# Logits of a two-layer decoder trunk: the products with the low half of the keys move from 64 to 128 rows, and the forget gates' bias rows move into them

## The chip, the core and the metric

The kernel runs on one core of one Trainium2 chip. The metric is the device time of one execution in microseconds. One execution in which every engine was recorded gives the profile; times in the rows below are microseconds from the start of its span.

## What is computed

Two layers over 512 tokens of width 1024, all in fp32. A layer sends `u = LN(x)*(1+scale)+shift` through one wide projection whose columns feed four mixers (pooling, a short convolution, and two attentions of four heads of 64 channels each), gates and sums their branch projections, projects once more, and adds an MLP of width 4096. The change concerns the logits of the two attentions:

```python
# MoBA: with 512 tokens, blocks of 256 and top 3, all past blocks are chosen: plain causal attention
logits = einsum('bhqd,bhkd->bhqk', rotary(q), rotary(k)) * 64 ** -0.5      # masked above the diagonal
# FoX: the same without rotary, plus a bias from the forget gates
cum = cumsum(log_sigmoid(u @ w_f + b_f))
logits = einsum('bhqd,bhkd->bhqk', q, k) * 64 ** -0.5 + cum[:, None] - cum[None, :]
p = softmax(logits); y = einsum('bhqk,bhkd->bhqd', p, v)
```

## The kernel before

**Products.** TensorE multiplies operands rounded to fp32r. To keep fp32's accuracy each operand is split into hi (rounded) and lo (the rest), and a product is three matmuls, hi*hi, hi*lo and lo*hi, into one PSUM bank: `mm3`, lines L128 to L130. `split` (L122 on ScalarE, L123 on VectorE) makes the halves.

**Order.** A layer's projections run tile by tile, 24 matmuls for 128 output columns. Between tiles, pieces of other work are emitted from Python generators: `between_step(rate)` takes the next piece of the attention or of the forget gates, `ada_step(rate)` the next piece of the modulation vectors (VectorE, L316 and L318). Layer by layer: first projections (queries and keys of MoBA, queries of FoX), values and rotary of MoBA, then tiles of convolution and pooling and the eight gate tiles of branch 0 with the MoBA attention between them; then FoX's values, forget gates and keys; then 16 gate tiles of branches 1 and 2 with the FoX attention between them; then branch 3, the output projection and the MLP. A scheduler orders each engine's instructions when the program is built, by the order in which they are written and by its own estimate of when operands and buffers are there; the queues then run in that order.

**Buffers.** Most tiles of 4 KB a partition come from one pool, `unit()`, of 24 buffers. A tile whose buffer is still read by older work waits.

**Logits.** `stack_queries` puts hi of a head's queries on the head's own 64 partitions and lo on the other 64. `stack_keys` puts hi of the keys on both halves, so that one matmul over 128 rows (L558) sums two of the three products. It puts lo of the keys on the head's own half only; one tile holds lo for two pairs of heads. The third product (L564) runs over 64 rows. A bf16 product of the identity and a mask (L559) adds the causal mask. In FoX a matmul over 32 rows (L562) adds the bias: `forget_rows` makes, for each head, 32 rows of which four hold the cumulated log gates and ones, for queries and for keys, by transposes into two PSUM banks and two copies (L684). Per tile of 128 queries of one head there are n = 256, 256, 384 and 512 key columns for the four query tiles. A layer has 16 such tiles in MoBA and 16 in FoX.

Behind a tile's logits stand the maximum (L566, VectorE), the exponential (L568, ScalarE), the normalization (L569, L571), transposes of the probabilities (L580, TensorE), their split, and the products with the values (L592, L593).

Of the kernel before, what the change touches and what calls it, by code (L numbers as in the profile page):

```python
# [30 lines left out]
UNITS = 24  # L31
# [9 lines left out]
EARLY_V = 0  # L41
# [26 lines left out]
def decoder_kernel(ctx, tc, x, c, positions, w_ada, b_ada, w_in, b_in, w_pool, pool_scale, conv_w,  # L68
# [5 lines left out]
    class Engine:  # L74
        """an engine whose instructions keep the order in which they are written while its letter is pinned"""
# [56 lines left out]
    def load(dst, src):  # L132
        """the loads of the start are issued in the order in which they are written, all others after them"""
        ins = nc.sync.dma_start(dst, src)
        if ordered[0]:
            tc.keep_in_program_order(ins)
            ordered[1] = ins.ins.name
        else:
            tc.add_manual_dep(ins.ins, ordered[1], mybir.DependencyInfo(
                mybir.DependencyClass.NoSync, mybir.DependencyReason.DATA), reason="after the start")  # L140
        return ins
# [25 lines left out]
    # silu(c), one column per k-tile  # L167
# [9 lines left out]
    def mean_rstd(xt, sums):  # L177
        """-mean and 1/std of the rows of xt, whose parts sum to sums"""
        nmean, rstd = small(), small()
        if len(sums) == 2:  # L180
            V.tensor_scalar(nmean, sums[0], sums[1], -1.0 / D, op0=ALU.add, op1=ALU.mult)  # L181
        else:
            V.tensor_scalar(nmean, sums[0], -1.0 / D, None, op0=ALU.mult)
        S.activation(t2(1024, BF16), xt, AF.Square, bias=nmean, accum_out=rstd)  # L184
        return nmean, rstd
# [5 lines left out]
    def statistics(xt, by_act):  # L191
        """mean, variance and 1/std of the rows of a tile"""
        if by_act:
            s0, mean, rstd = small(), small(), small()
            S.activation(t2(1024, BF16), xt, AF.Identity, scale=-1.0 / D, accum_out=s0)
            S.activation(t2(1024, BF16), xt, AF.Square, bias=s0, accum_out=rstd)
            V.tensor_scalar(mean, s0, -1.0, None, op0=ALU.mult)
            finish_rstd(rstd)
            return mean, rstd
        st, mv, rstd = small(12, "bn"), small(2, "mv"), small()  # L200
        for h in range(2):
            V.bn_stats(st[:, 6 * h:6 * h + 6], xt[:, HALF[h]])
        V.bn_aggr(mv, st.rearrange("p (a b) -> p a b", a=2))
        V.tensor_scalar(rstd, mv[:, 1:2], EPS, None, op0=ALU.add)
        G.tensor_tensor(rstd, rstd, mhalf, op=ALU.pow)
        return mv, rstd
# [25 lines left out]
    # per-partition columns of biases and scales  # L232
# [42 lines left out]
    # rotary tables  # L275
# [88 lines left out]
    # work that is emitted between the tiles of the projections  # L364
# [29 lines left out]
    def norm_tail(xt, gb, bb, ps):  # L394
        """xt <- LN(ALPHA * xt + psum) * gb + bb; returns the sums of its halves"""
        sums = [small(), small()]
        for h in range(2):
            cs = HALF[h]
            V.scalar_tensor_tensor(xt[:, cs], xt[:, cs], ALPHA, ps[h], op0=ALU.mult, op1=ALU.add,
                                   accum_out=sums[h])  # L400
        nmean, rstd = mean_rstd(xt, sums)
        t = unit()
        V.scalar_tensor_tensor(t, xt, nmean, gb, op0=ALU.add, op1=ALU.mult)
        finish_rstd(rstd)
        sums = [small(), small()]
        for h in range(2):
            cs = HALF[h]
            V.scalar_tensor_tensor(xt[:, cs], t[:, cs], rstd, bb[:, cs], op0=ALU.mult, op1=ALU.add,
                                   accum_out=sums[h])
        return sums  # L410
# [41 lines left out]
    def col_weights(w, c0, n=256):  # L452
        """hi/lo of n columns as n/128 stationary tiles, one at a time"""
        raw = load_raw((KD, n), [(lambda r: r, kcols(w, c0, n))])
        for j in range(n // P):
            t = whl((2, KD, P))
            split(t[:, 0], t[:, 1], raw[:, :, j * P:(j + 1) * P])
            yield t

    def project(w, tiles, evac, nh):  # L460
        """tiles: list of 256-wide column starts; evac(index of 128-tile, psum)"""
# [30 lines left out]
    def token_values(l, c0, n):  # L492
        """token-major projection of n columns (256 or 260) plus bias"""
# [26 lines left out]
    # for the logits of a head, hi and lo of its queries lie on the two halves of the partitions (hi on the head's own)  # L520
    # and hi of its keys on both: a pass over all partitions sums two of the three products
# [10 lines left out]
    def stack_keys(src, lo, bias=None):  # L532
        kt = unit((P, 2, T), F32R)
        for hh in range(2):
            own, other = OWN[hh], OWN[1 - hh]
            for half in (own, other):
                if bias is None:
                    S.copy(kt[half, hh], src[own])
                else:
                    S.activation(kt[half, hh], src[own], AF.Identity, bias=bias[own])  # L540
            if bias is None:
                V.tensor_tensor(lo[own], src[own], rd(kt[own, hh]), op=ALU.subtract)
            else:
                V.scalar_tensor_tensor(lo[own], src[own], bias[own], rd(kt[own, hh]), op0=ALU.add, op1=ALU.subtract)
        return kt, lo

    def attention(qk, v2, bias, ys):
        """causal attention of four heads, a piece for each step of the generator"""

        def logits(pr, hh, i):  # L550
            q, (kt, kl) = qk[pr], qk[2 + pr]
            h = 2 * pr + hh
            hp = slice(64 * hh, 64 * hh + 64)
# [6 lines left out]
            if bias is not None:  # L560
                hb = slice(32 * h, 32 * h + 32)
                TE.matmul(sps[:, :n], bias[0][hb, qc], bias[1][hb, :n], start=False, stop=False,  # L562
                          tile_position=(32 * h, 0))
            TE.matmul(sps[:, :n], q[hp, hh, qc], kl[hp, :n], start=False, stop=True)  # L564
# [20 lines left out]
        def values(pr, hh, half, pts, av):  # L585
            """the stationary operand is hi and lo of the values: the products of lo come out on the other partitions"""
# [48 lines left out]
    def forget_rows(z, cqk):  # L635
# [38 lines left out]
        V.tensor_copy(stq[:, :, :, 0], h4)  # L674
        V.tensor_tensor(stq[:, :, :, 1], c4, h4, op=ALU.subtract)
# [3 lines left out]
        res = unit((P, 2, T), F32R)  # L679
        for a in range(2):  # L680
            ps = bank("tr")
            for i in range(NT):
                TE.transpose(ps[:, i * P:(i + 1) * P], stg[:, a, i].rearrange("p h c -> p (h c)"), ident)
            S.copy(res[:, a], ps)  # L684
            cqk[a] = res[:, a]
            yield

# [53 lines left out]
    # ================= start =================  # L741
    def first_projection(w, tiles, evac):
        """K-outer projection of up to six 128-column tiles, each k-tile of u made on the way"""
# [6 lines left out]
        def load_ada(k0, g):  # L750
            """columns of g k-tiles of the shift and of the scale, all rows"""
# [122 lines left out]
    for l in range(DEPTH):  # L874
        pending += [ada_chunk(l, ch) for ch in (2, 3, 4)]
        # ---- MoBA projections, rotary and attention
        qk = [None] * 4

        qf2, klo = [None] * 2, [None]
# [8 lines left out]
        def rotate():  # L888
# [10 lines left out]
            for n, idx in enumerate(order):  # L899
# [13 lines left out]
                else:  # L913
                    if klo[0] is None:
                        klo[0] = unit((P, 2, T), F32R)
                    qk[idx] = stack_keys(qf, klo[0][:, idx - 2])
                yield

        fqk, fklo = [None] * 4, [None]

        def fox_evac(idx, ps):
# [4 lines left out]
            else:  # L926
                if fklo[0] is None:
                    fklo[0] = unit((P, 2, T), F32R)
                fqk[idx] = stack_keys(ps, fklo[0][:, idx - 2], cl[:, 14 + idx:15 + idx])
# [37 lines left out]
        # ---- pool  # L967
# [41 lines left out]
        # ---- conv: columns c_c, c_h, c_b  # L1009
# [38 lines left out]
        # ---- gates and branch projections  # L1048
# [35 lines left out]

        if EARLY_V:
            between_flush()
            v2, z = token_values(l, 2304, 260)
            cqk = [None, None]
            between.append(forget_rows(z, cqk))
# [3 lines left out]
        # ---- FoX projections and attention  # L1093
        between_flush()
        ada_rate[0] = ADA_IN
        if not EARLY_V:
            v2, z = token_values(l, 2304, 260)
            cqk = [None, None]
            between.append(forget_rows(z, cqk))
        project(w_in[l], [2048], lambda i, ps: fox_evac(i + 2, ps), 0)  # L1100
        between_flush()
        between.append(attention(fqk, v2, cqk, y_fox))
# [9 lines left out]
        # ---- W_o, norm, modulation of the MLP input  # L1112
# [10 lines left out]
        # ---- MLP  # L1123
# [78 lines left out]
```

## Time and profile before

| | us |
|---|---|
| three runs, lowest / median / highest | 1642.57 / 1645.42 / 1645.82 |
| span of the profiled execution, first to last instruction (nothing is shown around it) | 1642.6 |
| busy: TensorE matmuls / weight loads | 1609.2 (98%) / 1320.2 (80%) |
| busy: VectorE / ScalarE / GpSimd | 993.6 (60%) / 729.3 (44%) / 50.5 (3%) |

Matmuls overlap in the pipeline: a matmul's recorded duration is longer than the time for which it keeps the next one from starting. How much of the stream it takes is read from start to start. PE is TensorE, DVE is VectorE, ACT is ScalarE, POOL is GpSimd.

### The profile page before, as it was taken

How to read it: one execution, taken by the hardware profiler on the slowest of the kernel's cores; microseconds unless marked ns; L12 is line 12 of the kernel's file. 1: busy time of each engine (PE TensorE's matmuls, PEld its weight loads, DVE VectorE, ACT ScalarE, POOL GpSimd, SP SyncE). 2: the span in 40 equal slices, each digit the busy share in tenths (PEclk: the TensorE clock that was granted, in tenths of full speed). 3: DMA queues.
4: the chain of work that ended last, by engine and by line, in shares of the span. 5: the costliest groups of instructions: out<-in, count | busy, mean ns of one | idle time of the engine just before them, and what ended most of it. 6: DMA issues, size and time to landing. Idle time of an engine off the chain costs nothing.

```text
span 1642.6 us, 19902 instructions
## 1 busy us (share of the span) xinstructions
PE 1609.2 (98%) x7647; PEld 1320.2 (80%) x7647; DVE 993.6 (60%) x1629; ACT 729.3 (44%) x1210; POOL 50.5 (3%) x154
## 2 busy tenths in 40 slices
PE   5999999999999999999999999999999999999998
PEld 4877887778888888888888788777888988888886
DVE  7897455676675445744678835677567632265454
ACT  4565444443374434412375543554334643352231
POOL 1000000000010000000010000000000100000000
PEclk9999999999999999999999999999999999999999
DMA  9625222544536554222624222444226442332241
GB/s 318 187 75 177 81 87 82 181 129 135 200 108 193 167 166 154 103 79 101 241 92 151 95 90 65 148 147 146 73 83 231 141 123 83 103 103 94 86 180 51
DMA packets 151298, 215.54 MB, mean 131 GB/s; under 512 B 7564, under 2 KB 112991, under 8 KB 151203
## 3 DMA queue, kind: packets, MB, share of 16 engines
q1 hardware_dynamic: 148723, 206.84, 38.9%
q0 software_dynamic: 2176, 7.14, 1.1%
q8 instruction: 60, 0.98, 0.2%
q14 instruction: 35, 0.29, 0.1%
q10 hardware_dynamic: 304, 0.28, 0.1%
HBM read 205.33 MB, written 8.91 MB: 130 GB/s over the span
## 4 chain that ended last, share of the span: by engine, by line
PE 69%; issue 20%; DVE 4%; DMA 2%; ACT 2%; POOL 1%; SPq 0%; POOLq 0%; ACTq 0%; DVEq 0%
PE ps_mm L128 16%; PE ps_mm L130 16%; PE ps_mm L129 16%; PE ps_br L129 2%; PE ps_br L128 2%; PE ps_br L130 2%; PE ps_S L129 2%; PE ps_S L128 2%; PE ps_S L130 2%; PE ps_tr L130 2%; PE ps_tr L129 2%; PE ps_tr L128 2%; PE ps_S L564 1%; PE ps_tr L580 1%; DMA raw<-in_w_in_dram 1%
## 5 line engine op out<-in xcount | busy, mean ns | idle before, releaser
L128 PE MATMUL ps_mm<-uT,whl 128*128 128x512 f32 (+1 forms) x1280 | 492.3, 385 | 0.0
L130 PE MATMUL ps_mm<-uT,whl 128*128 128x512 f32 (+1 forms) x1280 | 487.4, 381 | 0.0
L129 PE MATMUL ps_mm<-uT,whl 128*128 128x512 f32 (+1 forms) x1280 | 486.9, 380 | 0.0
L123 DVE TENSOR_TENSOR whl<-raw,whl 128x1024 fp32r<-128x1024 f32 (+1 forms) x218 | 269.9, 1241 | 242.3 <-ACT whl L122 236.3
L122 ACT CAST whl<-raw 128x1024 fp32r<-128x1024 f32 (+1 forms) x218 | 229.9, 1058 | 180.9 <-PE ps_br L130 139.9
L130 PEld LDWEIGHTS ps_mm<-uT,whl 128*128 128x128 f32 x1280 | 240.9, 188 | 47.4
L128 PEld LDWEIGHTS ps_mm<-uT,whl 128*128 128x128 f32 x1280 | 241.1, 188 | 46.4 <-issue 0.7
L129 PEld LDWEIGHTS ps_mm<-uT,whl 128*128 128x128 f32 x1280 | 241.3, 189 | 45.1
L318 DVE SCALAR_TENSOR_TENSOR unit<-aw,scol,unit 128x512 f32<-128x512 f32 x148 | 110.8, 749 | 87.3 <-DMA aw<-in_w_ada_dram 86.4
L1067 ACT ACTIVATE t<-ps_mm,hgate 128x512 f32<-128x512 f32 x64 | 44.1, 690 | 202.2 <-PE ps_mm L130 202.2
L1128 ACT ACTIVATE t<-ps_mm,cols 128x512 f32<-128x512 f32 x62 | 42.7, 689 | 186.0 <-PE ps_mm L130 186.0
L716 DVE TENSOR_TENSOR raw<-raw,unit 128x1024 f32<-128x1024 f32 x80 | 94.6, 1219 | 11.3 <-DMA raw<-in_w_down_dram 5.9
L1075 DVE SCALAR_TENSOR_TENSOR t<-t,ps_br 128x512 f32<-128x512 f32 x48 | 33.0, 688 | 105.2 <-PE ps_br L130 100.1
L128 PE MATMUL ps_mm<-whl,unit 128*128 128x512 f32 x180 | 70.7, 392 | 0.0
L130 PE MATMUL ps_mm<-whl,unit 128*128 128x512 f32 x180 | 70.7, 392 | 0.0
L129 PE MATMUL ps_mm<-whl,unit 128*128 128x512 f32 x180 | 70.5, 392 | 0.0
L122 ACT CAST unit<-unit 128x512 fp32r<-128x512 f32 (+1 forms) x94 | 55.2, 613 | 32.0 <-DVE unit L123 31.8
L123 DVE TENSOR_TENSOR unit<-unit,unit 128x512 fp32r<-128x512 f32 (+1 forms) x94 | 61.8, 679 | 8.3 <-ACT unit L122 8.1
L184 ACT ACTIVATE t<-unit,s 128x1024 bf16<-128x1024 f32 x28 | 32.1, 1147 | 61.2 <-DVE s L181 55.5
L571 ACT ACTIVATE t<-t,s 128x128 f32<-128x128 f32 (+1 forms) x64 | 35.7, 563 | 32.4 <-DVE s L569 32.1
L130 PE MATMUL ps_br<-unit,whb 128*128 128x512 f32 x128 | 50.0, 390 | 0.0
L128 PE MATMUL ps_br<-unit,whb 128*128 128x512 f32 x128 | 49.9, 390 | 0.0
(275 smaller groups left out, 2577.6 us busy)
## 6 DMA issues: line engine op xcount, KB each, us to landing
raw<-in_w_in_dram SPq DMA_DIRECT2D x47, 1024.0 KB, 5.2
aw<-in_w_ada_dram SPq DMA_DIRECT2D x160, 256.0 KB, 2.8
raw<-in_w_up_dram SPq DMA_DIRECT2D x32, 1024.0 KB, 6.0
raw<-in_w_down_dram SPq DMA_DIRECT2D x32, 1024.0 KB, 4.8
unit<-in_w_ada_dram SPq DMA_DIRECT2D x32, 256.0 KB, 5.8
rawb<-in_w_branch_dram SPq DMA_DIRECT2D x32, 256.0 KB, 2.7
raw<-in_w_o_dram SPq DMA_DIRECT2D x8, 1024.0 KB, 4.9
xmid<-unit POOLq DMA_DIRECT2D x12, 512.0 KB, 2.9
```

Of the source, the lines that this page charges most:

```text
L122: S.copy(hi, src)
L123: V.tensor_tensor(lo, src, rd(hi), op=ALU.subtract)
L128: TE.matmul(ps, wh, ah, start=first, stop=False)
L129: TE.matmul(ps, wh, al, start=False, stop=False)
L130: last_mm[0] = TE.matmul(ps, wl, ah, start=False, stop=last)
L184: S.activation(t2(1024, BF16), xt, AF.Square, bias=nmean, accum_out=rstd)
L318: V.scalar_tensor_tensor(a, aw, scol[:, k:k + 1], a, op0=ALU.mult, op1=ALU.add)
L571: S.activation(pr_[:, :nv], pr_[:, :nv], AF.Copy, scale=sm)
L716: V.tensor_tensor(raw[:, k % 2], raw[:, k % 2], grow, op=ALU.mult)
L1067: S.activation(tg, ps, AF.Tanh, bias=hgate[l][:, n * KD + d:n * KD + d + 1], scale=0.5)
L1075: V.scalar_tensor_tensor(tg, tg, 1.0, bp, op0=ALU.add, op1=ALU.mult)
L1128: S.activation(r, ps, AF.Relu, bias=cl[:, B_UP + idx:B_UP + idx + 1])
```

## The change

Lo of the keys gets a tile of its own for each pair of heads, `(P, 2, T)`: for each head all 128 partitions. In MoBA lo is written on both halves, so L564 becomes a 128-row product of the stacked queries with it (which adds the product lo*lo). In FoX lo stays on the head's own half; the other half takes the four key-side bias rows of that head, and the remaining rows are zero or meet zeros. A second stacked tile of queries, `second`, holds hi of the queries on the head's own half and the query-side bias rows on the other half. L562 is left out. `forget_rows` therefore ends with twelve copies of 64 or 32 partitions and four memsets a layer instead of two copies, and it comes behind the keys (`while qk[3] is None: yield`; it was emitted there before, too). The pool gets 25 buffers; the scratch of GpSimd's DMA descriptors is set to 8192.

```diff
-UNITS = 24
+UNITS = 25
...
-    def stack_keys(src, lo, bias=None):
-        kt = unit((P, 2, T), F32R)
+    def stack_keys(src, bias=None):
+        kt, lo = unit((P, 2, T), F32R), unit((P, 2, T), F32R)
...
             if bias is None:
-                V.tensor_tensor(lo[own], src[own], rd(kt[own, hh]), op=ALU.subtract)
+                for half in (own, other):
+                    V.tensor_tensor(lo[half, hh], src[own], rd(kt[own, hh]), op=ALU.subtract)
             else:
-                V.scalar_tensor_tensor(lo[own], src[own], bias[own], rd(kt[own, hh]), op0=ALU.add, op1=ALU.subtract)
+                V.scalar_tensor_tensor(lo[own, hh], src[own], bias[own], rd(kt[own, hh]),
+                                       op0=ALU.add, op1=ALU.subtract)
...
-    def attention(qk, v2, bias, ys):
+    def attention(qk, v2, second, ys):
...
+            q2 = q if second is None else second[pr]
...
             TE.matmul(sps[:, :n], q[:, hh, qc], kt[:, hh, :n], start=True, stop=False)
             TE.matmul(sps[:, qc], identb, maskb, start=False, stop=False)
-            if bias is not None:
-                hb = slice(32 * h, 32 * h + 32)
-                TE.matmul(sps[:, :n], bias[0][hb, qc], bias[1][hb, :n], start=False, stop=False,
-                          tile_position=(32 * h, 0))
-            TE.matmul(sps[:, :n], q[hp, hh, qc], kl[hp, :n], start=False, stop=True)
+            TE.matmul(sps[:, :n], q2[:, hh, qc], kl[:, hh, :n], start=False, stop=True)
...
-    def forget_rows(z, cqk):
+    def forget_rows(z, qk, second):
...
-        V.tensor_copy(stq[:, :, :, 0], h4)
-        V.tensor_tensor(stq[:, :, :, 1], c4, h4, op=ALU.subtract)
+        for hh in range(2):
+            s2 = slice(2 - 2 * hh, 4 - 2 * hh)
+            V.tensor_copy(stq[:, :, s2, 0], h4[:, :, hh::2])
+            V.tensor_tensor(stq[:, :, s2, 1], c4[:, :, hh::2], h4[:, :, hh::2], op=ALU.subtract)
...
-        res = unit((P, 2, T), F32R)
+        while qk[3] is None:
+            yield
         for a in range(2):
             ps = bank("tr")
             for i in range(NT):
                 TE.transpose(ps[:, i * P:(i + 1) * P], stg[:, a, i].rearrange("p h c -> p (h c)"), ident)
-            S.copy(res[:, a], ps)
-            cqk[a] = res[:, a]
+            for pr in range(2):
+                if a == 0:
+                    second[pr] = unit((P, 2, T), F32R)
+                for hh in range(2):
+                    own, other = OWN[hh], OWN[1 - hh]
+                    if a == 0:
+                        S.copy(second[pr][own, hh], rd(qk[pr][own, hh]))
+                        S.copy(second[pr][other, hh], ps[other])
+                    else:
+                        lo = qk[2 + pr][1]
+                        r0 = other.start + 32 * pr
+                        r1 = other.start + 32 * (1 - pr)
+                        G.memset(rd(lo[r1:r1 + 32, hh]), 0.0)
+                        S.copy(lo[r0:r0 + 32, hh], ps[r0:r0 + 32])
             yield
...
-    nc = bacc.Bacc("TRN2", target_bir_lowering=False, num_devices=1)
+    nc = bacc.Bacc("TRN2", target_bir_lowering=False, num_devices=1, dynamic_dma_scratch_size=8192)
```

## Rows read from the trace of the kernel before

**Rows 1.** The page: busy time of TensorE, and its granted clock in 40 slices.
```profile
PE 1609.2 (98%) x7647; PEld 1320.2 (80%) x7647; DVE 993.6 (60%) x1629; ACT 729.3 (44%) x1210; POOL 50.5 (3%) x154
...
PEclk9999999999999999999999999999999999999999
```

**Rows 2.** The waits of TensorE: us in total, times, longest.
```profile
PE ps_tr L170 <- DMA cst<-in_consts_dram: 6.3, 1, 6.3
```

**Rows 3.** By source line, L562 and L564: count, ns minimum/median/maximum, forms.
```profile
L562 PE MATMUL ps_S<-unit x32: 377/408/498, 237.4 to 1150.7; 32*128 32x256 f32 x16, 32*128 32x384 f32 x8, 32*128 32x512 f32 x8
...
L564 PE MATMUL ps_S<-unit,unit x64: 379/410/500, 89.3 to 1151.1; 64*128 64x256 f32 x32, 64*128 64x384 f32 x16, 64*128 64x512 f32 x16
```

**Rows 4.** TensorE in order of time, first FoX logits: start, duration, line.
```profile
237.40 0.38 PE L562 MATMUL ps_S<-unit 32*128 32x256 f32 x1
237.71 0.38 PE L564 MATMUL ps_S<-unit,unit 64*128 64x256 f32 x1
238.03 0.50 PE L128 MATMUL ps_mm<-uT,whl 128*128 128x512 f32 x1
238.36 0.40 PE L129 MATMUL ps_mm<-uT,whl 128*128 128x512 f32 x1
```

**Rows 5.** TensorE in order of time, last FoX logits (fourth head).
```profile
1150.32 0.39 PE L558 MATMUL ps_S<-unit,unit 128*128 128x512 f32 x1
1150.55 0.23 PE L559 MATMUL ps_S<-maskb,identb 128*128 128x128 bf16 x1
1150.71 0.50 PE L562 MATMUL ps_S<-unit 32*128 32x512 f32 x1
1151.13 0.50 PE L564 MATMUL ps_S<-unit,unit 64*128 64x512 f32 x1
1151.56 0.39 PE L592 MATMUL ps_mm<-unit,unit 128*128 128x256 f32 x1
1151.79 0.28 PE L593 MATMUL ps_mm<-unit,unit 128*128 128x256 f32 x1
```

**Rows 6.** TensorE in order of time, last logits of FoX's third head.
```profile
1123.10 0.50 PE L562 MATMUL ps_S<-unit 32*128 32x512 f32 x1
1123.52 0.50 PE L564 MATMUL ps_S<-unit,unit 64*128 64x512 f32 x1
```

**Rows 7.** TensorE in order of time, second MoBA logits.
```profile
94.98 0.23 PE L559 MATMUL ps_S<-maskb,identb 128*128 128x128 bf16 x1
95.14 0.38 PE L564 MATMUL ps_S<-unit,unit 64*128 64x256 f32 x1
```

**Rows 8.** TensorE in order of time, first MoBA logits.
```profile
88.04 0.28 PE L558 MATMUL ps_S<-unit,unit 128*128 128x256 f32 x1
88.16 0.23 PE L559 MATMUL ps_S<-maskb,identb 128*128 128x128 bf16 x1
88.20 0.48 PE L128 MATMUL ps_mm<-uT,whl 128*128 128x512 f32 x1
88.52 0.39 PE L129 MATMUL ps_mm<-uT,whl 128*128 128x512 f32 x1
88.75 0.39 PE L130 MATMUL ps_mm<-uT,whl 128*128 128x512 f32 x1
```

**Rows 9.** ScalarE in order of time, ahead of the first FoX logits.
```profile
232.96 1.07 ACT L684 CAST unit<-ps_tr 128x512 fp32r<-128x512 f32 x2
235.96 0.69 ACT L1067 ACTIVATE t<-ps_mm,hgate 128x512 f32<-128x512 f32 x1 [1.93 <-PE ps_mm L130]
```

**Rows 10.** By source line, L542, lo of MoBA's keys.
```profile
L542 DVE TENSOR_TENSOR unit<-unit,unit x8: 676/683/691, 88.1 to 902.4; 64x512 fp32r<-64x512 f32 x8
```

**Rows 11.** One stretch: length, busy us of PE, PEld, DVE, ACT, POOL; clock, DMA.
```profile
115.00:125.00 10.00, 10.00 (x51) 8.00 (x50) 9.81 (x21) 6.31 (x12) 1.50 (x11) 1.00 0.10 26
```

**Rows 12.** The waits of GpSimd, the staging tile of the forget gates.
```profile
POOL unit L671 <- PE ps_S L564: 81.3, 2, 41.8
```

**Rows 13.** ScalarE in order of time, behind the last FoX logits.
```profile
1155.10 0.72 ACT L571 ACTIVATE t<-t,s 128x512 f32<-128x512 f32 x1 [1.22 <-DVE s L569]
```

More of the change, by code (lines that the diff above doesn't have):

```diff
@@ L40 @@
 V_RATE = 0.75
-EARLY_V = 0
 SOON = 2
@@ L541, in stack_keys @@
             if bias is None:
-                V.tensor_tensor(lo[own], src[own], rd(kt[own, hh]), op=ALU.subtract)
-            else:
-                V.scalar_tensor_tensor(lo[own], src[own], bias[own], rd(kt[own, hh]), op0=ALU.add, op1=ALU.subtract)
+                for half in (own, other):
+                    V.tensor_tensor(lo[half, hh], src[own], rd(kt[own, hh]), op=ALU.subtract)
+            else:
+                V.scalar_tensor_tensor(lo[own, hh], src[own], bias[own], rd(kt[own, hh]),
+                                       op0=ALU.add, op1=ALU.subtract)
         return kt, lo
-    def attention(qk, v2, bias, ys):
+    def attention(qk, v2, second, ys):
         def logits(pr, hh, i):
             q, (kt, kl) = qk[pr], qk[2 + pr]
-            h = 2 * pr + hh
-            hp = slice(64 * hh, 64 * hh + 64)
+            q2 = q if second is None else second[pr]
             nv = P * (i + 1)
@@ L877, in decoder_kernel @@
         qk = [None] * 4
-        qf2, klo = [None] * 2, [None]
+        qf2 = [None] * 2
         def rotary_evac(idx, ps):
@@ L913, in rotate @@
                 else:
-                    if klo[0] is None:
-                        klo[0] = unit((P, 2, T), F32R)
-                    qk[idx] = stack_keys(qf, klo[0][:, idx - 2])
+                    qk[idx] = stack_keys(qf)
                 yield
-        fqk, fklo = [None] * 4, [None]
+        fqk = [None] * 4
         def fox_evac(idx, ps):
@@ L926, in fox_evac @@
             else:
-                if fklo[0] is None:
-                    fklo[0] = unit((P, 2, T), F32R)
-                fqk[idx] = stack_keys(ps, fklo[0][:, idx - 2], cl[:, 14 + idx:15 + idx])
+                fqk[idx] = stack_keys(ps, cl[:, 14 + idx:15 + idx])
         def first_evac(idx, ps):
@@ L1083, in gates @@
                     between_step(ATT_RATE2)
[L1085 to L1089, printed above, removed]
         ada_rate[0] = ADA_G0
@@ L1095, in decoder_kernel @@
         ada_rate[0] = ADA_IN
[L1096 to L1099, printed above, removed]
+        v2, z = token_values(l, 2304, 260)
+        second = [None, None]
+        between.append(forget_rows(z, fqk, second))
         project(w_in[l], [2048], lambda i, ps: fox_evac(i + 2, ps), 0)
         between_flush()
-        between.append(attention(fqk, v2, cqk, y_fox))
+        between.append(attention(fqk, v2, second, y_fox))
         ada_rate[0] = ADA_FOX
```

## The prediction

> **What bounds the kernel now.** I read the page first. TensorE is busy for 98% of the span and its clock is in the top tenth in all forty slices [rows 1]: a faster clock has nothing to give. Busy time of overlapped matmuls proves little, so I read next what TensorE waits for. The longest of eight entries is 6.3 us, for the constants at the very start, and none of the eight stands on a line of the attention's logits [rows 2]. There TensorE streams without a named wait, and what is taken out of its stream comes out of the time, unless another engine becomes late.
>
> So the useful number is not a matmul's duration but its pitch, from its start to the start of the next. I read TensorE alone in order of time, around the logits. A plain 128-row product takes 0.12 us with 256 columns (88.04 to 88.16) and 0.23 us with 512 (88.52 to 88.75) [rows 8]; L558 with 512 takes the same 0.23 [rows 5]. The matmuls that the diff touches take much more. L562, over 32 rows, takes 0.31 us with 256 columns and 0.42 with 512; L564, over 64 rows, 0.32 and 0.43 [rows 4, 5]. That is 0.19 to 0.20 above the plain pitch at both widths, so the excess is paid for each instruction and not for columns. The next product pays as well: L592 takes 0.23 instead of 0.12 behind L564 [rows 5], L128 0.33 instead of 0.23 [rows 4]. The bf16 mask L559 ahead of a 64-row or 32-row matmul takes 0.16 [rows 5, 7]. There are 64 L564 (32 with 256 columns, 16 each with 384 and 512) and 32 L562 (16, 8 and 8) [rows 3].
>
> **The change part by part.** *lo of the keys over 128 rows (64 tiles).* After it L558, L559, L564 and the product behind them all use 128 rows; what is left is that L559 is bf16 between fp32 operands. The trace of before has this order once, by luck of the schedule: in the first tile of all the mask is followed by a 128-row L128. L559 then takes 0.04 us (88.16 to 88.20) and L128 takes 0.32 instead of 0.23, so 0.095 more, and the one after it is back at 0.23 [rows 8]. I price the new tile by that. L559: 0.16 becomes 0.04, 0.12 less. L564: an excess of 0.195 becomes 0.095, 0.10 less. The product behind: its excess of 0.10 goes. Where transposes follow, the view merges them and their excess can't be read; between 0 and 0.10 I take less there, and 0.08 over all tiles. That is 0.30 us a tile, 64 x 0.30 = 19.2 us. From below: if type and not rows caused the whole excess, L559 and L564 keep 0.16 and 0.195 and only the follower's 64 x 0.08 = 5.1 is saved. From above: if the 0.095 behind the mask is not paid either, 64 x 0.095 = 6.1 more.
>
> *The bias matmul (32 FoX tiles) goes.* 16 x 0.31 + 8 x 0.37 (between the two ends) + 8 x 0.42 = 11.3 us.
> Bias rows and lo rows lie in different row groups in half of the heads, and there they could have run side by side; in the third head (bias on rows 64 to 95, lo on 0 to 63) L562 takes 0.42 with 512 columns [rows 6], as it does in the fourth (96 to 127 against 64 to 127) [rows 5]. They don't overlap.
> The Trainium skill (TensorE: Matmul & The Clock Gate, "Part 3: Packing small matmuls") says that matmuls in distinct row groups run concurrently, some 4 ns apart. By it 16 of the 32 would cost about nothing and 5.6 us less would be saved; the starts of this trace disagree with it for these pairs.
>
> *VectorE.* Each MoBA key tile needs its lo on the other half too: 4 more L542 a layer at 0.683 us [rows 10], 5.5 us in both layers; four instructions on 16 columns cost next to nothing. Between 115 and 125 us VectorE is busy 9.81 of 10 us, and so is TensorE, 10.00 [rows 11]: this is the one stretch where cover is thin. What waits behind the added ones in VectorE's queue is the lo half of a weight tile, then TensorE's next tile. On the path between 0 and 5.5 us; the weight tiles are four deep, so I take 1 us.
>
> *ScalarE.* The two copies L684 of 128 x 512 out of PSUM, 0.535 us each [rows 9], become twelve a layer on 64 or 32 partitions: four of hi of the queries, four bias halves, four of 32 rows. At the same price 10 x 0.535 = 5.4 us a layer more. Before, the copies end at 234.0 and ScalarE then idles until L1067 at 235.96; the first FoX bias matmul starts at 237.40, with a gate tile on TensorE in between [rows 4, 9]. Four of the new copies depend on queries that are there long before and can go earlier; the other eight take 4.3 us where two took 1.1, and end 3.2 us later, at 237.2, about when the logits start. Behind them stand the gate's tanh and a later weight tile. Between 0 and 10.7 us over both layers; TensorE has the next gate tile to go on with, so I take 0.5 us. GpSimd's eight small memsets depend on nothing that is late, and nothing is queued behind them that is near; I cost them at nothing.
>
> *Buffers.* MoBA holds one buffer more, FoX two (lo of both pairs, second queries of both pairs in place of one tile of bias rows), and the pool has one more, paid for by the smaller scratch of GpSimd's DMA queue. That queue carries few transfers and I cost it at nothing. The pool is short already: the memset of the staging tile waits 81.3 us in two pieces for the last MoBA logits [rows 12]. It costs nothing as long as the attention's pieces, one to a gate tile, are not late.
>
> Sum: -19.2 - 11.3 + 1.5 = -29.0 us. The profiled execution's span is 1642.6, and that makes 1613.6; the median of the runs is 1645.4, 2.8 us above the span, and that makes 1616.4. I predict the middle, 1615.
>
> **The rivals.** *Type, not rows.* The switch from bf16 to fp32 alone could cost what L564 shows; for it speaks that every L564 but one follows a bf16 mask, against it the one pair of [rows 8]. Saved: 5.1 + 11.3 - 1.5 = 14.9, so about 1629.
> *Cover gone.* The stretch of [rows 11] and the copies of [rows 9] come onto the path in full: 5.5 + 10.7 = 16.2 given back of 30.5, about 1630. Against it: weight tiles are four ahead, and TensorE can take other work.
> *Row groups overlap after all:* half of the 11.3 us of bias matmuls was free, 5.6 us less is saved, about 1620. The change would then not remove what it seems to.
> *Slower: the pool.* FoX takes one buffer more than the pool gains. If a tile of probabilities can't be allocated until the tiles before it are read, logits, softmax, transpose and values of a piece run bare at the end of the gates. A piece's logits end at 1151.56 and the scaled probabilities at 1155.82 [rows 5, 13], 4.3 us. Seven such bare pieces of 32 give back 30 us; with eight in one layer and six in the other the time is 1615 + 60 = 1675, with seven it is about 1645. For it speaks the wait of [rows 12]; against it, that pieces come one to a gate tile, which is 30 products of 0.23 us or 6.9 us without them, so a piece's delay is free until the gates run out.
>
> **How the numbers follow.** My forecast has 0.70, type 0.11, cover gone 0.08, overlap 0.03: faster by more than 0.2% (3.3 us, about what these runs can tell from no change) in all of these, 0.92. The pool: 0.02 that it just cancels the gain, 0.06 that it is slower. The forecast alone spans 1606 (the 6.1 us from above and 1.5 of costs that don't come) to 1621; up to 1630 the range takes in overlap and the middles of type and of cover gone. Left out are their far halves and the pool, some two in ten with what I have not thought of.
>
> **What would show it.** No L562. L559 at 0.04 us and L564 at the plain pitch plus 0.095, the product behind at its plain pitch: right. L559 at 0.16 and L564 unchanged: type. If those pitches come out and the time is 10 us off, look for TensorE waiting for lo of weights near 100 to 130 us or 900 to 930, or for the copies before the first FoX logits. If the last FoX logits come later against the gate tiles than now, it is the pool. My sum is wrong above all if the single pair of [rows 8] isn't typical.

## Result, and the profile after

The changed kernel takes 1623.22 us (median of four runs: 1626.41, 1619.73, 1621.39, 1625.04) where the kernel before took 1644.78 beside it: a ratio of 0.9867 [0.985, 0.9885], 21.6 us less. Forecast were 1615 us and 29.0 less; the time lies in the range of 1606 to 1630. The two runs near 1626 have a mean granted clock of 0.995, the two near 1620 one of 0.998; the profiled execution is the longest of the four.

The page of the changed kernel, its parts 1 and 2, against [rows 1]:

```profile
span 1624.6 us, 19880 instructions
...
PE 1584.3 (98%) x7615; PEld 1309.9 (81%) x7615; DVE 994.4 (61%) x1641; ACT 740.4 (46%) x1230; POOL 54.8 (3%) x162
...
PEclk9999999999999999999999999999999999999999
```

TensorE has 32 matmuls fewer (7647 to 7615) and is busy for 98% of a shorter span, as before. The clock's row looks untouched; one slice of it hides something, as a later view shows.

The changed kernel's TensorE in order of time, in three places: the first FoX logits against [rows 4], a stretch in the second layer, and the last FoX logits against [rows 5]:

```profile
234.87 0.28 PE L560 MATMUL ps_S<-unit,unit 128*128 128x256 f32 x1
234.99 0.23 PE L561 MATMUL ps_S<-maskb,identb 128*128 128x128 bf16 x1
235.82 0.39 PE L562 MATMUL ps_S<-unit,unit 128*128 128x256 f32 x1 [0.60 <-ACT unit L700]
236.05 0.39 PE L127 MATMUL ps_mm<-uT,whl 128*128 128x512 f32 x1
...
1070.12 0.39 PE L128 MATMUL ps_mm<-uT,whl 128*128 128x512 f32 x1
1073.84 0.58 PE L591 MATMUL ps_mm<-unit,unit 128*128 128x256 f32 x1 [3.33 <-DVE unit L122]
...
1077.42 0.63 PE L128 MATMUL ps_mm<-uT,whl 128*128 128x512 f32 x1
1077.85 0.63 PE L129 MATMUL ps_mm<-uT,whl 128*128 128x512 f32 x1
...
1132.98 0.39 PE L560 MATMUL ps_S<-unit,unit 128*128 128x512 f32 x1
1133.21 0.23 PE L561 MATMUL ps_S<-maskb,identb 128*128 128x128 bf16 x1
1133.25 0.48 PE L562 MATMUL ps_S<-unit,unit 128*128 128x512 f32 x1
1133.57 0.28 PE L590 MATMUL ps_mm<-unit,unit 128*128 128x256 f32 x1
1133.68 0.28 PE L591 MATMUL ps_mm<-unit,unit 128*128 128x256 f32 x1
```

(L560 is the old L558, L561 the mask, L562 now the product with lo of the keys, L590 and L591 the old L592 and L593; L127 to L129 are the old L128 to L130.) Read the last five rows first, start to start: the mask takes 0.04 us where it took 0.16, L562 takes 0.32 where the old pair of L562 and L564 took 0.85, and L590 behind it takes the plain 0.11 instead of 0.23. Then the other two places: TensorE now waits, once for 0.60 us and once for 3.33, and behind the longer wait the products' pitch is 0.43 us (1077.42 to 1077.85) instead of 0.23.

I summed such pitches over all 64 logits tiles of both traces, from the starts. In us:

| | before | after |
|---|---|---|
| L558 / L560 | 11.21 | 11.20 |
| mask, L559 / L561 | 10.12 | 4.12 |
| bias, old L562 | 11.28 | none |
| lo, L564 / new L562 | 22.71 | 15.89 |
| excess of the product behind | 5.50 | 0.18 |
| sum | 60.82 | 31.40 |

The logits take 29.4 us less; the prediction had 30.5. Two of the 64 masks, ahead of the first FoX logits of each layer, take 0.84 and 0.87 us instead of 0.04, since L562 waits behind them (0.60 us of idle time in the rows above). These 1.6 us are in the 4.12; without them the logits take 31.0 us less. The profiled executions differ by less, 1642.6 to 1624.6, which is 18.0. So 11.4 us were lost in that execution outside the logits; the next views show where.

TensorE and VectorE in the waits of the changed kernel (total, times, longest):

```profile
PE ps_mm L591 <- DVE unit L122: 3.3, 1, 3.3
PE ps_S L562 <- ACT unit L700: 1.2, 2, 0.6
...
DVE unit L317 <- DMA aw<-in_w_ada_dram: 98.1, 70, 4.5
```

The first two are new. L317 is the adaLN modulation step that the planner puts between the tiles; it works on tiles `aw` of the weights, which arrive by DMA in two buffers. The changed kernel's VectorE at the 3.3 us:

```profile
1067.45 0.75 DVE L317 SCALAR_TENSOR_TENSOR unit<-aw,scol,unit 128x512 f32<-128x512 f32 x1 [1.52 <-DMA aw<-in_w_ada_dram]
1068.12 0.68 DVE L122 TENSOR_TENSOR unit<-t,unit 64x512 fp32r<-64x512 f32 x1
1068.72 0.74 DVE L317 SCALAR_TENSOR_TENSOR unit<-aw,scol,unit 128x512 f32<-128x512 f32 x1
1071.04 0.75 DVE L317 SCALAR_TENSOR_TENSOR unit<-aw,scol,unit 128x512 f32<-128x512 f32 x1 [1.58 <-DMA aw<-in_w_ada_dram]
1071.71 0.68 DVE L1086 SCALAR_TENSOR_TENSOR t<-t,ps_br 128x512 f32<-128x512 f32 x1
1072.31 0.55 DVE L564 TENSOR_REDUCE s<-ps_S 128x1 f32<-128x384 f32 x1
1072.77 0.68 DVE L1087 TENSOR_TENSOR unit<-unit,t 128x512 f32<-128x512 f32 x1
1073.37 0.41 DVE L122 TENSOR_TENSOR unit<-ps_tr,unit 128x256 fp32r<-128x256 f32 x1
```

Follow it backwards from L591 at 1073.84. It needs the last row, the split of the probabilities. That one waited for nothing of its own: it stands in VectorE's queue behind L1087, L564 and L1086, and these (L564 is the maximum of a later tile, the other two add a gated branch) behind modulation steps, two of which waited 1.52 and 1.58 us for their tiles. The windows of the changed kernel around it (us, busy us of PE, PEld, DVE, ACT, POOL, clock, DMA share, GB/s):

```profile
1068.00:1072.00 4.00, 2.51 (x13) 1.60 (x12) 2.42 (x5) 1.30 (x4) 0.20 (x1) 1.00 0.43 131
1072.00:1076.00 4.00, 2.16 (x7) 1.76 (x8) 4.00 (x10) 2.37 (x6) 0.20 (x1) 0.64 0.23 67
1076.00:1080.00 4.00, 4.00 (x13) 3.25 (x12) 2.60 (x5) 1.10 (x2) 0.35 (x2) 0.51 0.32 84
1080.00:1084.00 4.00, 4.00 (x23) 3.31 (x22) 1.50 (x3) 1.93 (x3) 0.00 (x0) 1.00 0.88 274
```

Toward the end of the idle 3.33 us the granted clock goes to its lower level (0.51 in the third row) and is back in the fourth; it is at half for 6.83 us, from 1073.09 to 1079.92. TensorE works again from 1073.84, so 6.08 us of work run at half speed and 3.0 us are lost. A slice of the page is 40.6 us wide, and 6.83 us at half lower its mean only to about 0.92, which prints as 9: the forty slices don't show such a dip.

Stall and clock make 6.4 of the 11.4. The rest can be placed by matching the two traces matmul by matmul (the n-th of a line against the n-th of the same line) and reading how the lag grows: the start is 1.0 us later; the two MoBA stretches together come out only 7.2 us shorter where their pitches give about 9.7, so some 2.5 us are lost there; some 1.5 us are spread in pieces too small to name.

The 1.6 us of waits ahead of the first FoX logits have another cause. The changed kernel's ScalarE there, against [rows 9]:

```profile
230.40 2.51 ACT L693 CAST unit<-unit 64x512 fp32r<-64x512 f32 x4
232.81 2.36 ACT L694 CAST unit<-ps_tr 64x512 fp32r<-64x512 f32 x4
235.19 2.36 ACT L700 CAST unit<-ps_tr 32x512 fp32r<-32x512 f32 x4
237.58 0.69 ACT L1078 ACTIVATE t<-ps_mm,hgate 128x512 f32<-128x512 f32 x1
```

Twelve copies run in one block. The four of the queries (L693) were ready long before, but ran directly ahead of the bias copies and pushed these back by 2.4 us.

### The profile page after: what moved, and what is told of

Its sections match the earlier page's. It is cut to its first block, busy times and chain, and to the rows that moved or that the text cites. A ratio compares the mean times of both kernels' runs of the same rounds, so it can differ in the third digit from the quotient of the medians.

```text
span 1624.6 us, 19880 instructions
## 1 busy us (share of the span) xinstructions
PE 1584.3 (98%) x7615; PEld 1309.9 (81%) x7615; DVE 994.4 (61%) x1641; ACT 740.4 (46%) x1230; POOL 54.8 (3%) x162
## 4 chain that ended last, share of the span: by engine, by line
PE 63%; issue 21%; DVE 8%; DMA 3%; ACT 3%; POOL 1%; SPq 1%; POOLq 0%; DVEq 0%; ACTq 0%
PE ps_mm L129 15%; PE ps_mm L127 14%; PE ps_mm L128 14%; PE ps_br L128 2%; PE ps_br L127 2%; PE ps_br L129 2%; PE ps_S L127 2%; PE ps_S L129 2%; PE ps_S L128 2%; PE ps_tr L129 2%; PE ps_tr L128 2%; PE ps_tr L127 2%; DMA aw<-in_w_ada_dram 1%; DVE whl L122 1%; DVE unit L122 1%
## 5 line engine op out<-in xcount | busy, mean ns | idle before, releaser
L127 PE MATMUL ps_mm<-uT,whl 128*128 128x512 f32 (+1 forms) x1280 | 491.6, 384 | 0.0
L129 PE MATMUL ps_mm<-uT,whl 128*128 128x512 f32 (+1 forms) x1280 | 488.7, 382 | 0.3 <-DVE whl L122 0.3
L128 PE MATMUL ps_mm<-uT,whl 128*128 128x512 f32 (+1 forms) x1280 | 487.4, 381 | 0.0
L129 PEld LDWEIGHTS ps_mm<-uT,whl 128*128 128x128 f32 x1280 | 241.6, 189 | 48.1 <-DVE whl L122 0.8
L128 PEld LDWEIGHTS ps_mm<-uT,whl 128*128 128x128 f32 x1280 | 241.8, 189 | 45.4
L127 PEld LDWEIGHTS ps_mm<-uT,whl 128*128 128x128 f32 x1280 | 241.7, 189 | 44.3
L317 DVE SCALAR_TENSOR_TENSOR unit<-aw,scol,unit 128x512 f32<-128x512 f32 x148 | 110.8, 748 | 99.2 <-DMA aw<-in_w_ada_dram 98.1
L1086 DVE SCALAR_TENSOR_TENSOR t<-t,ps_br 128x512 f32<-128x512 f32 x48 | 32.9, 686 | 83.9 <-PE ps_br L129 80.4
L127 PE MATMUL ps_mm<-whl,unit 128*128 128x512 f32 x180 | 70.7, 392 | 0.0
L129 PE MATMUL ps_mm<-whl,unit 128*128 128x512 f32 x180 | 70.7, 392 | 0.0
L128 PE MATMUL ps_mm<-whl,unit 128*128 128x512 f32 x180 | 70.5, 392 | 0.0
L188 POOL TENSOR_TENSOR s<-s,mhalf 128x1 f32<-128x1 f32 x30 | 17.2, 575 | 1026.7 <-DVE s L187 1022.1
L129 PE MATMUL ps_br<-unit,whb 128*128 128x512 f32 x128 | 50.0, 390 | 0.0
L127 PE MATMUL ps_br<-unit,whb 128*128 128x512 f32 x128 | 49.9, 390 | 0.0
```

What stands on the lines that cost most here:

```text
L127: TE.matmul(ps, wh, ah, start=first, stop=False)
L128: TE.matmul(ps, wh, al, start=False, stop=False)
L129: last_mm[0] = TE.matmul(ps, wl, ah, start=False, stop=last)
L317: V.scalar_tensor_tensor(a, aw, scol[:, k:k + 1], a, op0=ALU.mult, op1=ALU.add)
L1086: V.scalar_tensor_tensor(tg, tg, 1.0, bp, op0=ALU.add, op1=ALU.mult)
```

## The experiments

Theory of the sizes: the rows of the old matmuls cost what the prediction says, and the 8 us by which the result falls short of the logits' 29.4 are for the most part VectorE's queue held by `aw` and the clock behind it; the copies cost the 1.6 us of waits. The rivals: the type of the mask, the pool, and cover that is gone in other places. Ratios below are against the kernel before on the same chip. None of the kernels leaves work out.

**A third `aw` buffer in the changed kernel.**
```diff
-AW_BUFS = 2
+AW_BUFS = 3
```


> The changed kernel with a third buffer for the weight slices of the modulation vectors (aw), nothing else. Theory A: the 3.5 us stall of TensorE near 1070 us comes from VectorE's queue, held by a modulation step that waits for its DMA; with a slice more loaded ahead the wait of VectorE for aw shrinks to below half, the stall goes, TensorE's clock stays up there, and the time falls by 3 to 7 us below the changed kernel, to about 1617. Theory B: the stall is the pool of unit buffers; then this changes nothing beyond the noise of 2 us, and the stall stays.

Measured: 1615.29 us, 0.9824 [0.9811, 0.9838]. VectorE of this kernel at the place of the stall, its window and its wait:

```profile
1069.26 2.42 DVE L317 SCALAR_TENSOR_TENSOR unit<-aw,scol,unit 128x512 f32<-128x512 f32 x3
1071.72 0.69 DVE L1086 SCALAR_TENSOR_TENSOR t<-t,ps_br 128x512 f32<-128x512 f32 x1
```

```profile
1072.00:1076.00 4.00, 4.00 (x21) 3.30 (x20) 3.34 (x7) 1.56 (x5) 0.00 (x0) 1.00 1.05 350
```

```profile
DVE unit L317 <- DMA aw<-in_w_ada_dram: 48.2, 40, 4.6
```

Three modulation steps follow each other without a wait, TensorE is busy throughout, the clock stays up. Both parts of the loss went with the transfer's wait. Matched matmul by matmul, this kernel gains 5.5 us on the changed one in the second FoX stretch (6.4 at the stall, of which 0.9 are lost again behind it), but also 4.6 us before 70 us, which has nothing to do with the logits. The next run tells how much of that the kernel before has as well.

**The third buffer in the kernel before** (with the changed kernel's smaller scratch, so that it fits).
```diff
-AW_BUFS = 2
+AW_BUFS = 3
...
```


> The kernel before with a third buffer for the weight slices of the modulation vectors, and the smaller DMA scratch that makes room. It tells how much of the 8 us that the third buffer gave to the changed kernel has nothing to do with the change. Theory A (the stall near 1070 us belongs to the changed kernel's order of VectorE's queue; the gain of some 4 us before 70 us belongs to either kernel): 3 to 5 us faster than before, all of it before 70 us. Rival: the kernel before loses as much to modulation steps as the changed one, in many small waits; then it gains 7 to 9 us, spread over the attention stages.

Measured: 1640.54 us, 0.9976 [0.9967, 0.9985], and all of the 4.1 us come before 70 us. The kernel before at its start, VectorE and TensorE:

```profile
55.77 0.42 DVE L123 TENSOR_TENSOR whb<-rawb,whb 128x256 fp32r<-128x256 f32 x1 [2.72 <-ACT whb L122]
```

```profile
56.68 0.58 PE L86 MATMUL ps_tr<-ones,unit 128*128 128x2 f32 x4 [1.48 <-DVE unit L86]
```

There, too, an instruction that waits holds VectorE's queue (L123 stands behind ScalarE's copy of a branch weight, and that copy behind the weight's own DMA, not one of `aw`); with three buffers the order is another and this wait is absent. The clock has a part in it here as well: in the kernel before it is at its lower level for 3.41 us behind this wait, from 58.86, which costs 1.7 of the 4.1 us; with three buffers it stays up. (That part depends on the execution: with two buffers, 24 units and FoX alone, both below, wait 1.04 and 1.05 us there and keep the clock up.) A window of the kernel before:

```profile
60.00:62.00 2.00, 2.00 (x6) 1.51 (x6) 2.00 (x5) 0.00 (x0) 0.00 (x0) 0.50 0.23 42
```

So with three buffers on both sides the change is worth 1640.5 − 1615.3 = 25.2 us, and 3.6 of the missing microseconds (by medians) went with the third buffer: the stall and the clock behind it, which cost 6.4 in the profiled execution and, by the clocks of the four runs, less in two of them.

**Four buffers.**
```diff
-AW_BUFS = 2
+AW_BUFS = 4
```


> The changed kernel with four weight slice buffers. Theory A: with three buffers VectorE still waits 48 us for slices and TensorE loses 1.1 us at one place near 1088 us; a fourth shortens the wait again and gives 0.5 to 1.5 us on the run with three. If three are already enough, the same time within 1 us.

Measured: 1614.98 us, 0.9826 [0.9813, 0.984]. VectorE's wait for `aw` falls from 48.2 to 25.5 us and the time stays: what is left of the wait is hidden.

**The pool: one unit more, one less.**
```diff
-UNITS = 25
+UNITS = 26
```


> The changed kernel with 26 unit buffers instead of 25. Theory B (the pool is short by what FoX holds more): the stall near 1070 us goes and 3 to 7 us are gained. Theory A (a modulation step waiting for its DMA holds VectorE): the steps start no later than now, VectorE's wait for aw stays at 60 us or more, and the time is within 3 us of the changed kernel.

```diff
-UNITS = 25
+UNITS = 24
```


> The changed kernel with the 24 unit buffers of before. Theory A (stalls come from instructions in VectorE's queue that wait for a DMA): within 2 us of the changed kernel, with the stall near 1070 us as it is. Theory B (the pool is short, and the 25th buffer pays for what the change holds): 5 us or more slower than the changed kernel, with the FoX tiles late.

Measured: 1620.29 us, 0.9859 [0.9845, 0.9872], and 1622.15 us, 0.9864 [0.985, 0.9877]. Both intervals hold the changed kernel's ratio, and the stall is still there, with 2.77 and 2.82 us. TensorE with 26 units and with 24:

```profile
1071.92 0.39 PE L591 MATMUL ps_mm<-unit,unit 128*128 128x256 f32 x1 [2.77 <-DVE unit L122]
```

```profile
1070.39 0.58 PE L591 MATMUL ps_mm<-unit,unit 128*128 128x256 f32 x1 [2.82 <-DVE unit L122]
```

The pool is neither the cause of the loss nor does it cost anything.

**Type or rows: the mask in fp32 in the kernel before.**
```diff
-    identb = cp.tile([P, P], BF16, name="identb")
-    maskb = cp.tile([P, P], BF16, name="maskb")
+    identb = cp.tile([P, P], F32R, name="identb")
+    maskb = cp.tile([P, P], F32R, name="maskb")
...
```


> The kernel before, with identity and mask of the mask product in fp32r instead of bf16 (and the smaller DMA scratch, to make room). All products of the logits then have one type; rows stay 128, 128, 32, 64. Rows theory: L562 and L564 keep 0.31 to 0.43 us and the product behind keeps its 0.10 more; only the mask changes, and the time stays within 5 us of before. Type theory: L564 falls to the plain 0.12 to 0.23 us in MoBA, and 6 to 15 us are gained.

Measured: 1645.12 us, 1.000 [0.9991, 1.0009]. TensorE of this kernel:

```profile
96.49 0.22 PE L559 MATMUL ps_S<-maskb,identb 128*128 128x128 f32 x1
96.64 0.38 PE L564 MATMUL ps_S<-unit,unit 64*128 64x256 f32 x1
96.95 0.50 PE L128 MATMUL ps_mm<-uT,whl 128*128 128x512 f32 x1
97.29 0.39 PE L129 MATMUL ps_mm<-uT,whl 128*128 128x512 f32 x1
```

No type changes here any more, and the pitches hardly move: 0.15 for the mask ahead of 64 rows, 0.31 for the 64 rows, 0.34 for the product behind. Rows cost it. (The smaller scratch of GpSimd's queue, in this kernel too, costs nothing either.)

**The same in the changed kernel**: could the 0.085 us that are left behind the mask be had?


> The changed kernel with identity and mask in fp32r instead of bf16: all logits products over 128 rows and of one type. If the 0.085 us that the last product still pays behind the mask is the switch from bf16 to fp32, it goes, and the mask itself costs 0.055 (its 128 columns) to 0.11 us (the pitch of 128-column transposes) instead of 0.04: between 4.5 us gained and 1 us gained over 64 tiles. If it is something else (a new stationary operand that isn't loaded ahead), nothing is gained or 4 us are lost.

Measured: 1625.45 us, 0.9883 [0.9867, 0.9898]. TensorE of this kernel:

```profile
95.31 0.22 PE L561 MATMUL ps_S<-maskb,identb 128*128 128x128 f32 x1
95.36 0.34 PE L562 MATMUL ps_S<-unit,unit 128*128 128x256 f32 x1
95.54 0.39 PE L127 MATMUL ps_mm<-uT,whl 128*128 128x512 f32 x1
```

The mask goes from 0.039 to 0.059 us, L562's excess from 0.085 to 0.053 (medians): a tile pays 0.112 us instead of 0.124, or 0.8 us less over 64 tiles, and the time doesn't fall. Most of the excess moves, it doesn't go. What it is, if not the change of type, I don't know.

This run shows something else. It has no stall of L591, with two `aw` buffers and both parts of the change in; TensorE waits at another place, in the first layer, for the same reason. VectorE and TensorE of this kernel:

```profile
289.36 0.75 DVE L317 SCALAR_TENSOR_TENSOR unit<-aw,scol,unit 128x512 f32<-128x512 f32 x1 [2.00 <-DMA aw<-in_w_ada_dram]
```

```profile
291.00 1.11 PE L578 MATMUL ps_tr<-cst,t 128*128 128x128 f32 x4 [2.17 <-ACT t L569]
```

L569, the normalization, needs a reciprocal of VectorE's that stood behind this modulation step. The clock goes to its lower level here too, for 3.41 us from 290.78.

**MoBA alone and FoX alone.** In the first, the kernel before gets lo on both halves in MoBA, 25 units and the smaller scratch; in the second, the changed kernel keeps 64 rows in MoBA.
```diff
...
-                V.tensor_tensor(lo[own], src[own], rd(kt[own, hh]), op=ALU.subtract)
+                for half in (own, other):
+                    V.tensor_tensor(lo[half, hh], src[own], rd(kt[own, hh]), op=ALU.subtract)
...
+            if bias is None:
+                TE.matmul(sps[:, :n], q[:, hh, qc], kl[:, hh, :n], start=False, stop=True)
...
```


> The kernel before with MoBA's part of the change alone: lo of MoBA's keys on both halves, L564 over 128 rows there, FoX as before with its 32-row and 64-row matmuls, 25 buffers and the smaller scratch. By the pitches of the changed kernel 32 tiles save 0.29 us each, 9.3 us. If VectorE's four more instructions a layer come onto the path in the stretches where it is full (85 to 135 and 880 to 930 us), 3 to 7 us are left; if they are covered, 8.5 to 9.5.

```diff
...
-            TE.matmul(sps[:, :n], q2[:, hh, qc], kl[:, hh, :n], start=False, stop=True)
+            hp = slice(0, P) if second is not None else OWN[hh]
+            TE.matmul(sps[:, :n], q2[hp, hh, qc], kl[hp, hh, :n], start=False, stop=True)
```


> The changed kernel with MoBA's lo of the keys back on the head's own half and L564 there over 64 rows; FoX as changed. By the pitches 32 FoX tiles save 0.63 us each, 20.1 us in all. If the loss of 8 us against the forecast sits in FoX's stretch alone, this is 12 to 13 us faster than before, and with MoBA's part alone (8.1 us) the two add up to the whole change. If the loss comes from both parts together (VectorE's added work in MoBA), this is 17 to 20 us faster.

Measured: MoBA alone 1636.39 us, 0.9952 [0.9939, 0.9964], 8.1 less where the pitches give 9.85. FoX alone 1624.97 us, 0.9893 [0.9879, 0.9906], 17.9 less where they give 19.7, with the two waits in them. Added up that is 26.0, and both together give 21.6: 4.4 us more are lost when both parts are in, a rough number, as each of the three differences is known to 2 or 3 us. Neither of the two has the stall of L591. TensorE's waits in FoX alone, which has no entry for L591:

```profile
PE ps_tr L424 <- ACT unit L418: 3.9, 7, 0.6
PE ps_S L562 <- ACT unit L700: 1.2, 2, 0.6
```

The waits before the first FoX logits belong to FoX's part; the stall shows in neither part alone.

**Fewer modulation steps in the second FoX stretch.**
```diff
-ADA_FOX = 2.2
+ADA_FOX = 1.8
```


> The changed kernel with 1.8 modulation steps to a gate tile in FoX's stretch instead of 2.2, two weight slice buffers as before. Theory A': a gate tile with FoX pieces became some 0.6 us shorter, while each step's slice still has to be loaded behind the step that frees its buffer, so VectorE waits longer for slices and is late for TensorE. Then fewer steps to a tile shorten VectorE's waits for slices between 1020 and 1130 us, the stall near 1070 us goes, and the time is 3 to 6 us below the changed kernel. Rival: the stall is an accident of the order at one place; then a stall of 1 us or more turns up at another place, and the time stays within 2 us.

Measured: 1626.2 us, 0.9905 [0.9891, 0.9918], which is slower than the changed kernel; neither theory expected that. The stall went, and matched matmul by matmul the second layer gains 12.3 us on the kernel before where the changed kernel gains 6.0. The first layer lost it again, at the end of its gates and in its norm. TensorE of this kernel:

```profile
415.74 0.50 PE L330 MATMUL ps_br<-unit,ones 128*128 128x512 f32 x1 [1.96 <-DVE unit L122]
...
451.97 1.09 PE L424 MATMUL ps_tr<-cst,unit 128*128 128x128 f32 x8 [1.85 <-ACT unit L418]
```

The steps that no longer fit between the tiles are done at the end, where TensorE waits for them. This pace is no remedy; the buffer is.

**The query copies earlier, with three buffers.** The four copies of hi of the queries move to the start of the forget gates' work.
```diff
-AW_BUFS = 2
+AW_BUFS = 3
...
+        for pr in range(2):
+            second[pr] = unit((P, 2, T), F32R)
+            for hh in range(2):
+                S.copy(second[pr][OWN[hh], hh], rd(qk[pr][OWN[hh], hh]))
...
-                if a == 0:
-                    second[pr] = unit((P, 2, T), F32R)
...
-                        S.copy(second[pr][own, hh], rd(qk[pr][own, hh]))
```


> The changed kernel with the third weight slice buffer, and with the four copies of hi of FoX's queries written at the start of the forget gates' work instead of behind the keys. If the two waits of 0.8 us before the first FoX logits come from these four copies, which stand ahead of the bias copies in ScalarE's queue though their data are there long before, the waits go and the time is 1 to 2 us below the run with the third buffer alone, about 1613.5. If the copies cost elsewhere what they save here (ScalarE is wanted for the splits of weights), nothing is gained.

Measured: 1616.45 us, 0.983 [0.9816, 0.9843], against 0.9824 without the edit. ScalarE and TensorE of this kernel:

```profile
220.52 2.51 ACT L639 CAST unit<-unit 64x512 fp32r<-64x512 f32 x4
```

```profile
228.18 1.06 PE L690 MATMUL ps_tr<-cst,unit 128*128 128x128 f32 x8 [1.09 <-DVE unit L682]
```

The two waits of L562 are gone, and the transposes of the forget rows wait instead, 1.1 to 1.3 us in each layer. The 2.5 us of copies now stand ahead of the gates' own chain through ScalarE and VectorE, which the transposes end.

## Why the prediction was right, and by how much it was off

*What bounds the kernel.* Right: of the 29.4 us that left TensorE's stream, 21.6 came out of the time, and with the third buffer on both sides 25.2. One thing was read too quickly: *a faster clock has nothing to give*. The forty slices of [rows 1] hide the 3.41 us at the lower level near 60 us, 1.7 us of the kernel before.

*Lo over 128 rows.* Right in mechanism and nearly in size. The single pair of [rows 8] was typical: the mask takes 0.039 us (forecast 0.04), L562's excess is 0.085 (0.095), and nothing is left behind it (0.003 a tile, 0 forecast). The three terms were 0.12, 0.10 and 0.08 a tile, 19.2 us; measured are 6.0 + 6.8 + 5.3 = 18.1, the old L564 and the new L562 side by side, and 7.6 + 6.8 + 5.3 = 19.7 without the two waits of L562, which count as masks. *Type, not rows* is refuted by the mask in fp32 in the kernel before.

*The bias matmul.* 11.3 forecast, 11.28 measured. *Row groups overlap* is refuted with it: nothing of the 11.28 had been free.

*The costs are the term that was mis-sized.* I took 1.5 us. Against the 31.0 us that the pitches give without the waits, they were 9.4 by the medians and 13.0 in the profiled execution: 6.4 stall and clock, 2.5 in MoBA's stretches, 1.6 copies, 1.0 at the start, 1.5 without a name. Three things were wrong in it:
- VectorE at 1 us. I looked for thin cover in MoBA's stretch of [rows 11]. Some 2.5 us were lost in the two layers' MoBA stretches (1.7 by the medians with MoBA alone: 8.1 of 9.85); that VectorE caused it is not shown. The larger loss came in the second layer's FoX stretch, where VectorE's queue was held by a transfer. The wait on `aw` was in the trace of before, 86.4 us in all, and I took it for free because no TensorE wait hung on it. The third buffer shows that this was the cause.
- The clock. I didn't ask what a stall would do to it. It nearly doubled the price of the stall: 3.0 us behind 3.3.
- The copies at 0.5 us, since four of them could go earlier. They didn't, and the waits behind them cost 1.6. Moving them by hand doesn't pay either, as it holds up the chain that makes the other eight.

*Cover gone* was thus right in kind, in part, and wrong in place for the most. That the time still lies in the range is partly luck: the forecast alone was to span 1606 to 1621, and 1623.2 lies in the part above, which was there for the rivals. *The pool* is refuted by 26 and by 24 units.

What stays open: why the stall appears at L591 when both parts are in. Each part shifts the order of VectorE's queue a little, and together they put the split behind two late steps. The fp32 mask in the changed kernel speaks for an accident of the order, as there the same kind of wait strikes at 291 us instead; what decides the place is not shown. That the two longer of the four runs are those with the dip of the clock fits their means of 0.995, but one of them alone was profiled. And the 2.5 us of MoBA's stretches and some 1.5 us of small losses have no known cause.

## What to carry to other kernels

Read the pitch from start to start, and look through the trace for a place where the planned order already occurs: one pair of rows priced 64 tiles to within 3%, once waits were taken out. Then ask of each engine's queue which instruction waits for a transfer, how long, and what of TensorE's stands behind it: work that is paced per tile comes closer together when the tiles get shorter, while its transfers may not get faster. A deeper buffer for it costs one line, and should be tried with the change and, for a fair comparison, without it.

## What the hardware showed that was not expected

A matmul over 32 or 64 rows among 128-row ones takes 0.19 to 0.20 us more than a 128-row one, at 256 and at 512 columns alike and with either type of mask (0.31 and 0.42 us of pitch, where 128 rows take 0.12 and 0.23); the 128-row product behind it takes 0.10 more, and the mask ahead of it 0.09 more in fp32 and 0.12 in bf16. The Trainium skill (TensorEngine Tiling (Array Packing), "Key Properties") says that a change of the tiling mode drains TensorE. These prices are in line with it: they stand on both sides of each change in the number of rows; that it is a drain, no row shows.

Around the end of 3.33 us without work the granted clock went to its lower level, 1.2 GHz, and stayed there for 6.83 us, though TensorE was busy 4.00 of 4.00 us in that time (1076 to 1080), and then rose to 2.4 GHz. With the fp32 mask in the changed kernel it did so for 3.41 us around the end of 2.17 us without work.
